# Retention transposes of keys, values and outputs gathered: one group for both heads of a pair, two PSUM tiles at a time

## The chip, the cores and the metric

The kernel runs on one core of one Trainium2 chip. The metric is the device time of one launch in microseconds (us). Three runs of the kernel before took 2369.28, 2370.20 and 2370.94 us; the median is 2370.2 us.

## The reference, cut to what matters

Two layers of a recurrent decoder run over 320 tokens at once: a prompt of 256 and 8 sequences of 8. Each layer normalises x, projects it with one wide matrix, runs three branches on the result (a diagonal state space model, a gated linear recurrence, a retention), multiplies each by its gate, projects and merges them. The change lies in the retention alone, which works in chunks of 128 tokens:

```
def step(r, inp):                       # one chunk; 8 heads of 128
    qc, kc, vc = inp
    sc = einsum('bihd,bjhd->bhij', qc, kc) * dmask
    inner = einsum('bhij,bjhe->bihe', sc, vc)
    cross = einsum('bihd,bhde->bihe', qc, r) * xi
    r_new = r * g_chunk + einsum('bjhd,bjhe->bhde', kc * zeta, vc)
    return r_new, inner + cross
# then each head's output is normalised over its 128 channels and multiplied by gn_g
y_ret = o * silu(z_ret)                 # goes into the next projection
```

The projections leave keys and values with channels on the partitions. The sums over tokens need tokens there, and so keys, values and, after the normalisation, outputs are transposed on TensorE (PE).

## The kernel before, in words

**The main stream.** All projections are one stream of matmuls, written out by `stream` (L1310). A weight chunk of 512 x 256 comes by DMA into `raw`; `prep` (L1339) splits half a chunk into a high part `whi` on ScalarE (ACT, L125) and a rest `wlo` on VectorE (DVE, L98); each 128 x 128 block is then multiplied three times (L1436 to L1438), accumulating in a PSUM tile `pt`. One half chunk is a step: 12 matmuls of 320 columns. `whi` and `wlo` have four buffers each, and `prep` is three steps ahead in the stages told of here, so the split of a step can begin only when PE has finished the step that held its buffer.

**The side work.** Everything else is written as Python generators. After each step `self.step()` lets them write their next piece into the same five in-order queues (PE, DVE, ACT, GpSimd called POOL, and SP, which issues nearly all DMAs). `yield` lets a generator rest one step and go on in the one after; `yield 0` goes on at once, unless the modelled load of DVE or ACT has run too far ahead (`BEHIND`). Which instructions stand beside which is thus fixed when the program is built.

**PSUM.** `pt` has two buffers of two banks. All side work shares four banks of [128, 512] (`ps()`, L181, pool `pside`): the tiles take the four in turn. A tile can be written only when every reader of the tile four before it is done, whichever of the two was written into the queues first.

**The retention** of a layer goes by four pairs of heads, m = 0 to 3. `ret_qk` (L884) rotates q and k: a copy with swapped halves comes back by DMA as `rsw`. `ret_heads` (L955) multiplies keys with queries into two side tiles (L973 to L977), DVE masks them into `scs` and `rsc` (L982 to L988), the keys of each head are transposed (L997) and scaled by DVE into `rkt` (L1000), the keys of the sample group likewise (`rp4`, `rkz`). `ret_v` (L910) transposes the values. Then come score times value, the normalisation, and the transposes of the outputs (`ron`, L1079), one head and then the other, with a yield between. `ret_state` (L1089) updates the states `r0` with matmuls L1112 and a DVE instruction each (L1116).

Of the kernel before, what the change touches and what calls it, by code (L numbers as in the profile page):

```python
# [15 lines left out]
OP = mybir.AluOpType  # L16
# [24 lines left out]
K_ZP, K_ZS, K_GP, K_G2, K_LO = 0, 16, 24, 48, 72  # L41
# [37 lines left out]
class Program:  # L79
# [830 lines left out]
    def ret_v(self, l, m, pt):  # L910
        nc = self.nc
        v = self.wt([128, 2, T], name="rv")
        self.mul(v, pt[:, :, :T], self.rs2())
        yield
        vd = self.vt([128, 2, 2, 64], name="rvd")
        self.copy(vd, v[:, :, None, SEQ:].to_broadcast([128, 2, 2, 64]))
        yield
        v4 = self.parts_of(v)
        yield
        vt = self.wt([128, 2, 2, 128], name="rvt")  # L920
        vs = self.vt([128, 2, 128], name="rvs")
        for n in range(2):
            p = self.ps()
            for c in range(2):
                nc.tensor.transpose(p[:, c * 128:(c + 1) * 128], v[:, n, c * 128:(c + 1) * 128], self.ident)
            nc.tensor.transpose(p[:, 256:384], vd[:, n].rearrange("p r t -> p (r t)"), self.ident)
            yield
            self.copy(vt[:, n].rearrange("p c e -> p (c e)"), p[:, :256])
            self.copy(vs[:, n], p[:, 256:384])
        p = self.rows_of(v4)  # L930
        yield
        v4 = self.wt([128, 512], F32R, name="rv4")
        self.copy(v4, p)
        self.stt(v4, v4.bitcast(F32), self.sm[:, K_LO + 1:K_LO + 2], p, OP.mult, OP.add)
        v4 = v4.rearrange("p (n c e) -> p n c e", n=2, c=2)
        self.ret['v', m] = (vt, vs, v4)
        self.flag['v', l, m] = True
# [17 lines left out]
    def ret_heads(self, l, m):  # L955
        nc, I, O, sm = self.nc, self.I, self.O, self.sm
# [8 lines left out]
        q, k = self.ret.pop(('q', m)), self.ret.pop(('k', m))  # L965
# [3 lines left out]
        k4 = self.parts_of(k)  # L969
        pp, sc = [], []  # L970
        for n in range(2):
            p = self.ps()
# [3 lines left out]
        p = pp[0][:, 384:]  # L976
# [3 lines left out]
        for n in range(2):  # L980
            r = slice(n * 64, n * 64 + 64)
# [3 lines left out]
        for n in range(2):  # L985
            t = self.vt([128, 384], name="rsc")
# [3 lines left out]
            yield 0  # L990
        kt = self.wt([128, 2, 2, 128], name="rkt")
        kz = self.wt([128, 2, 256], name="rkz")
        for n in range(2):
            h = 2 * m + n
            p = self.ps()
            for c in range(2):
                nc.tensor.transpose(p[:, c * 128:(c + 1) * 128], k[:, n, c * 128:(c + 1) * 128], self.ident)  # L997
            yield
            for c in range(2):
                self.ts(kt[:, n, c], p[:, c * 128:(c + 1) * 128],  # L1000
                        sm[:, K_ZP + 2 * h + c:K_ZP + 2 * h + c + 1], OP.mult)
        p = self.rows_of(k4)
        yield
        for n in range(2):
            h = 2 * m + n
            self.ts(kz[:, n], p[:, n * 256:n * 256 + 256], sm[:, K_ZS + h:K_ZS + h + 1], OP.mult)
        yield 0
        k4 = self.wt([128, 2, 256], F32R, name="rk4")
# [5 lines left out]
        for n in range(2):  # L1014
            r = self.rt([128, NB, 128], name="r0")
# [5 lines left out]
        vt, vs, v4 = self.ret.pop(('v', m))  # L1021
        po = []
        mv = self.pl.tile([128, 2, 3, 2], F32, name="mv", tag="mv")
        for n in range(2):
            p = self.ps()
# [28 lines left out]
        v, rs, t = (vv[:, i] for i in range(3))  # L1054
# [8 lines left out]
        on = []  # L1063
# [8 lines left out]
        while not self.flag.get(('zr', l, m)):  # L1072
            yield
        z = self.szr.pop(m)
        for n in range(2):
            h = 2 * m + n
            p = self.ps()
            for s in range(3):
                nc.tensor.transpose(p[:, s * 128:(s + 1) * 128], on[n][:, s], self.ident)  # L1079
            g = self.pcol(l, 'gn', h)  # L1080
            yield
            self.stt(z[:, n, :SEQ], p[:, :256], g, z[:, n, :SEQ], OP.mult, OP.mult)
            zs = z[:, n, SEQ:].rearrange("p (g s) -> p g s", g=4)
            self.stt(zs, p[:, 256:384].rearrange("p (g s) -> p g s", g=4)[:, :, :2 * NS], g, zs, OP.mult, OP.mult)
            yield
        yield 0
        self.y_parts(l, 1, m, z)

    def ret_state(self, l, m, kt, k4, vt, v4, r0):  # L1089
# [468 lines left out]
```

## Time and profile before

| | before |
|---|---|
| median of three runs | 2370.2 us |
| profiled execution, own time | 2368.96 us |
| its span, first to last instruction | 2367.2 us |
| PE busy | 2347.3 us, 99% |
| DVE busy | 1535.7 us, 65% |
| ACT busy | 1107.2 us, 47% |
| POOL busy | 605.7 us, 26% |

PE is busy nearly all the time, and the chain of waits that ended last runs over PE for 97% of the span. The retention stages lie at about 417 to 690 us (layer 0) and 1590 to 1870 us (layer 1). A matmul's row tells its start and a modelled length; matmuls overlap, so what one costs is the distance between starts.

### The profile page before, as it was taken

The numbers are of one execution on the slowest core, as the hardware profiler recorded it, in microseconds if no ns is written. First come the engines' busy times: TensorE is split into PE (matmuls) and PEld (weight loads), VectorE is DVE, ScalarE is ACT, GpSimd is POOL, SyncE is SP. The second block draws the span as 40 slices with busy tenths as digits, with TensorE's granted clock in tenths as the row PEclk, the third lists the DMA queues.
The fourth block names the chain that finished last, engine by engine and source line by source line (L and its number), as shares of the span: only waits on it lengthen the run. The fifth ranks groups of instructions, "written<-read, shape, count | busy, mean of one in ns | idle before, by whom it ended". The sixth has DMA issues, their size and how long they took to land.

```text
span 2367.2 us, 44419 instructions
## 1 busy us (share of the span) xinstructions
PE 2347.3 (99%) x16778; PEld 2323.5 (98%) x16778; DVE 1535.7 (65%) x2830; ACT 1107.2 (47%) x2021; POOL 605.7 (26%) x1159
## 2 busy tenths in 40 slices
PE   9999999999999999999999999999999999999997
PEld 9999999999999999999999999999999999999997
DVE  7886668676665657656557765856676656555544
ACT  6645644444443444344455564444444334444443
POOL 2020008999430000300100000699950300000011
PEclk9999999999999999999999999999999999999999
DMA  6745785455545545455646577454555554444453
GB/s 234 219 151 164 195 236 173 137 193 188 176 161 193 164 151 171 146 165 189 202 158 188 164 217 219 144 170 153 170 179 194 180 174 162 149 152 145 158 178 129
DMA packets 154311, 413.72 MB, mean 175 GB/s; under 512 B 18800, under 2 KB 60528, under 8 KB 153840
## 3 DMA queue, kind: packets, MB, share of 16 engines
q1 hardware_dynamic: 153664, 410.38, 54.6%
q8 instruction: 132, 2.16, 0.4%
q14 instruction: 83, 0.68, 0.1%
q10 hardware_dynamic: 432, 0.50, 0.1%
HBM read 373.83 MB, written 31.74 MB: 171 GB/s over the span
## 4 chain that ended last, share of the span: by engine, by line
PE 97%; DVE 2%; DMA 1%; ACT 0%; issue 0%; SPq 0%; DVEq 0%; ACTq 0%
PE pt L1436 30%; PE pt L1438 30%; PE pt L1437 30%; PE ps L679 1%; PE ps L806 1%; DVE wlo L98 1%; PE ps L582 1%; DMA raw<-w_in 0%; PE ps L1040 0%; PE ps L1112 0%; PE ps L1096 0%; PE ps L952 0%; PE ps L973 0%; PE ps L1079 0%; PE ps L671 0%
## 5 line engine op out<-in xcount | busy, mean ns | idle before, releaser
L98 DVE TENSOR_TENSOR wlo<-raw,whi 128x512 fp32r<-128x512 f32 (+1 forms) x1199 | 857.5, 725 | 746.0 <-ACT whi L125 735.7
L125 ACT ACTIVATE whi<-raw 128x512 fp32r<-128x512 f32 (+1 forms) x1199 | 744.8, 629 | 1019.2 <-PE pt L1437 847.0
L1436 PE MATMUL pt<-xh,whi 128*128 128x320 f32 x3352 | 1049.6, 313 | 1.5 <-ACT whi L125 1.0
L1437 PE MATMUL pt<-xl,whi 128*128 128x320 f32 x3352 | 1036.1, 309 | 0.8 <-DVE xl L118 0.7
L1438 PE MATMUL pt<-xh,wlo 128*128 128x320 f32 x3352 | 1036.5, 309 | 0.2 <-DVE wlo L98 0.2
L1436 PEld LDWEIGHTS pt<-xh,whi 128*128 128x128 f32 x3352 | 629.8, 188 | 7.5 <-issue 3.9
L1437 PEld LDWEIGHTS pt<-xl,whi 128*128 128x128 f32 x3352 | 630.0, 188 | 4.2 <-DVE xl L118 1.5
L1438 PEld LDWEIGHTS pt<-xh,wlo 128*128 128x128 f32 x3352 | 629.5, 188 | 0.8 <-DVE wlo L98 0.6
L1438 PE MATMUL pt<-yhl,wlo 128*128 128x320 f32 x768 | 237.4, 309 | 2.8 <-DVE wlo L98 2.8
L1436 PE MATMUL pt<-yhl,whi 128*128 128x320 f32 x768 | 238.1, 310 | 0.0
L1437 PE MATMUL pt<-yhl,whi 128*128 128x320 f32 x768 | 237.3, 309 | 0.0
L599 POOL TENSOR_TENSOR cs<-H,l2r 128x64 f32<-128x64 f32 x254 | 136.0, 535 | 239.2 <-DVE H L112 219.5
L271 POOL TENSOR_TENSOR acc<-acc,sq 128x320 f32<-128x320 f32 x28 | 25.6, 913 | 590.8 <-ACT sq L125 589.8
L1436 PE MATMUL pt<-M,whi 128*128 128x320 f32 x512 | 158.4, 309 | 0.0
L1438 PE MATMUL pt<-M,wlo 128*128 128x320 f32 x512 | 158.2, 309 | 0.0
L1437 PE MATMUL pt<-M,whi 128*128 128x320 f32 x512 | 158.2, 309 | 0.0
L1438 PEld LDWEIGHTS pt<-yhl,wlo 128*128 128x128 f32 x768 | 144.2, 188 | 3.1 <-DVE wlo L98 3.1
L1436 PEld LDWEIGHTS pt<-yhl,whi 128*128 128x128 f32 x768 | 144.2, 188 | 0.2
L1437 PEld LDWEIGHTS pt<-yhl,whi 128*128 128x128 f32 x768 | 144.2, 188 | 0.0
L600 POOL TENSOR_TENSOR cs<-H,l2i 128x64 f32<-128x64 f32 x254 | 131.8, 519 | 0.0
L601 POOL TENSOR_TENSOR cs<-cs,H 128x64 f32<-128x64 f32 x254 | 117.9, 464 | 0.0
L602 POOL TENSOR_TENSOR H<-cs,cs 128x64 f32<-128x64 f32 x254 | 107.8, 424 | 19.9
(258 smaller groups left out, 2445.5 us busy)
## 6 DMA issues: line engine op xcount, KB each, us to landing
raw<-w_in SPq DMA_DIRECT2D x447, 512.0 KB, 4.3
raw<-w_out SPq DMA_DIRECT2D x64, 512.0 KB, 4.3
raw<-wb_lru SPq DMA_DIRECT2D x32, 512.0 KB, 5.0
raw<-wb_ret SPq DMA_DIRECT2D x32, 512.0 KB, 3.7
raw<-wb_s SPq DMA_DIRECT2D x32, 512.0 KB, 3.6
r<-sret SPq DMA_DIRECT2D x16, 512.0 KB, 7.6
ret_s<-r SPq DMA_DIRECT2D x16, 512.0 KB, 3.0
raw<-w_glu SPq DMA_DIRECT2D x16, 512.0 KB, 3.5
```

The costliest lines, as they stand in the source:

```text
L98: self.nc.vector.tensor_tensor(o, a, b, op=op)
L125: self.nc.scalar.activation(o, a, f, **k)
L271: self.nc.gpsimd.tensor_tensor(self.acc, self.acc, sq, op=OP.add)
L582: self.nc.tensor.matmul(pp[g][:, a * HN:(a + 1) * HN], wst[:, a, g * 128:(g + 1) * 128], ust[:, 2 * a + g], start=True, stop=True, skip_gr ...
L599: g.tensor_tensor(t1, old, lr, op=OP.mult)
L600: g.tensor_tensor(t2, self.swap(old), li, op=OP.mult)
L601: g.tensor_tensor(t1, t1, new, op=OP.add)
L602: g.tensor_tensor(new, t1, t2, op=OP.add)
L679: nc.tensor.matmul(o[q * 32:(q + 1) * 32], w[:, c, m], H[:, q0 + m, c, col:col + HN], start=col == 1 and c == 0, stop=c == 1, tile_positio ...
L1436: nc.tensor.matmul(o, wh[:, cs], xh, start=k == 0, stop=False)
L1437: nc.tensor.matmul(o, wh[:, cs], xl, start=False, stop=False)
L1438: nc.tensor.matmul(o, wl[:, cs], xh, start=False, stop=k == nk - 1)
```

## The change

The values of both heads go into one PSUM tile and their sample rows into a second, allocated together; the keys of both heads go into one tile, and the sample keys into a second, written right behind; the outputs of both heads go into two tiles in one group. The reads stand behind one yield in place of two or three. No arithmetic changes: the same 24 transposes per pair. The copies of the values to SBUF become one of 512 and one of 256 columns, from two of 256 and two of 128.

```
         vs = self.vt([128, 2, 128], name="rvs")
-        for n in range(2):
-            p = self.ps()
-            for c in range(2):
-                nc.tensor.transpose(p[:, c * 128:(c + 1) * 128], v[:, n, c * 128:(c + 1) * 128], self.ident)
-            nc.tensor.transpose(p[:, 256:384], vd[:, n].rearrange("p r t -> p (r t)"), self.ident)
-            yield
-            self.copy(vt[:, n].rearrange("p c e -> p (c e)"), p[:, :256])
-            self.copy(vs[:, n], p[:, 256:384])
+        p, pd = self.rows_of(v), self.ps()
+        for n in range(2):
+            nc.tensor.transpose(pd[:, n * 128:(n + 1) * 128], vd[:, n].rearrange("p r t -> p (r t)"), self.ident)
+        yield
+        self.copy(vt.rearrange("p n c e -> p (n c e)"), p)
+        self.copy(vs.rearrange("p n e -> p (n e)"), pd[:, :256])
+        yield
         p = self.rows_of(v4)
...
-        for n in range(2):
-            h = 2 * m + n
-            p = self.ps()
+        pk, p = self.rows_of(k), self.rows_of(k4)
+        yield
+        for n in range(2):
             for c in range(2):
-                nc.tensor.transpose(p[:, c * 128:(c + 1) * 128], k[:, n, c * 128:(c + 1) * 128], self.ident)
-            yield
-            for c in range(2):
-                self.ts(kt[:, n, c], p[:, c * 128:(c + 1) * 128],
-                        sm[:, K_ZP + 2 * h + c:K_ZP + 2 * h + c + 1], OP.mult)
-        p = self.rows_of(k4)
-        yield
+                i = 2 * (2 * m + n) + c
+                self.ts(kt[:, n, c], pk[:, n * 256 + c * 128:n * 256 + (c + 1) * 128],
+                        sm[:, K_ZP + i:K_ZP + i + 1], OP.mult)
+            yield 0
...
-        for n in range(2):
-            h = 2 * m + n
-            p = self.ps()
+        pp = [self.ps(), self.ps()]
+        for n in range(2):
             for s in range(3):
-                nc.tensor.transpose(p[:, s * 128:(s + 1) * 128], on[n][:, s], self.ident)
-            g = self.pcol(l, 'gn', h)
-            yield
+                nc.tensor.transpose(pp[n][:, s * 128:(s + 1) * 128], on[n][:, s], self.ident)
+        yield
+        for n in range(2):
+            p, g = pp[n], self.pcol(l, 'gn', 2 * m + n)
             self.stt(z[:, n, :SEQ], p[:, :256], g, z[:, n, :SEQ], OP.mult, OP.mult)
...
-            yield
-        yield 0
+            yield 0
+        yield
         self.y_parts(l, 1, m, z)
```

**On PE, third pair (m = 2) of layer 0, before.** From the score products to the sample keys; `ps_` tiles are side tiles in the order in which they take the four banks, and the main matmuls between are left out.

```order
L973 MATMUL ps_7343<-ra_6962,ra_7141 128x256 [waits DVE_49]
L973 MATMUL ps_7346<-ra_6962,ra_7141 128x256 [waits PE_49]
...
L1112 MATMUL ps_7368<-vbd_5307,rk4_6823 128x512
...
L1112 MATMUL ps_7419<-vbd_5307,rk4_6823 128x512 [waits DVE_49,PE_49]
...
L997 MATMUL ps_7441<-ident_507,ra_7141 128x128 [waits DVE_49,PE_49]
...
L925 MATMUL ps_7462<-ident_507,rv_7318 128x128 [waits DVE_49]
...
L997 MATMUL ps_7489<-ident_507,ra_7141 128x128 [waits DVE_49]
```

The keys of the two heads (L997) stand two steps apart, each with a tile of its own, and the values (L925) between them. Tile 7441 takes the bank of 7343, and 7462 that of 7346.

**The same place after** (L951 are transposes by `rows_of`, L924 those of the sample values, L972 the score products, L1108 the state matmuls).

```order
L972 MATMUL ps_7376<-ra_6952,ra_7132 128x256
L972 MATMUL ps_7379<-ra_6952,ra_7132 128x256 [waits PE_49]
...
L1108 MATMUL ps_7383<-vbd_5307,rk4_6817 128x512 [waits PE_49]
...
L951 MATMUL ps_7432<-ident_507,ra_7132 128x128 x4
L951 MATMUL ps_7437<-ident_507,rp4_7373 128x128 [waits DVE_49,PE_49,Activation_49]
...
L1108 MATMUL ps_7443<-vbd_5307,rk4_6817 128x512 [waits DVE_49]
...
L951 MATMUL ps_7463<-ident_507,rv_7312 128x128 [waits DVE_49]
L951 MATMUL ps_7463<-ident_507,rv_7312 128x128 x3
L924 MATMUL ps_7468<-ident_507,rvd_7353 128x128 [waits DVE_49]
```

Both heads' keys, the sample keys and a state matmul now stand in one group, two steps behind the score products, and the values one step behind that. In turns of four, 7437 takes the bank of 7376, 7443 that of 7379, 7463 that of 7383, and 7468, the sample values, that of 7432, the keys.

**On DVE, the same place, before:** the masking of the scores and the first scaling of keys (`rkt`), with the splits `wlo` of the main stream between.

```order
L98 TENSOR_TENSOR rsc_7393<-ps_7343,rdm_7212 128x128
L98 TENSOR_TENSOR wlo_7397<-raw_7320,whi_7396 128x512
L98 TENSOR_TENSOR rsc_7412<-ps_7346,rdm_7212 128x256
L98 TENSOR_TENSOR rsc_7412<-ps_7346,rdm_7212 128x128
L118 SCALAR_TENSOR_TENSOR r0_6828<-r0_6828,ps_7368 128x512
L98 TENSOR_TENSOR wlo_7424<-raw_7320,whi_7423 128x512
L98 TENSOR_TENSOR wlo_7445<-raw_7370,whi_7444 128x512
L118 SCALAR_TENSOR_TENSOR r0_6828<-r0_6828,ps_7419 128x512
L98 TENSOR_TENSOR wlo_7472<-raw_7370,whi_7471 128x512
L112 TENSOR_SCALAR rkt_7439<-ps_7441,sm_508 128x128 x2
```

Two instructions read a tile of keys, four steps' splits after the scores.

**The same place after.**

```order
L98 TENSOR_TENSOR rsc_7424<-ps_7376,rdm_7200 128x256
L98 TENSOR_TENSOR rsc_7424<-ps_7376,rdm_7200 128x128
L98 TENSOR_TENSOR rsc_7427<-ps_7379,rdm_7200 128x256
L98 TENSOR_TENSOR rsc_7427<-ps_7379,rdm_7200 128x128
L118 SCALAR_TENSOR_TENSOR r0_6822<-r0_6822,ps_7383 128x512
L98 TENSOR_TENSOR wlo_7446<-raw_7355,whi_7445 128x512
L98 TENSOR_TENSOR wlo_7475<-raw_7355,whi_7474 128x512
L112 TENSOR_SCALAR rkt_7430<-ps_7432,sm_508 128x128 x4
```

The four readings of the keys' tile stand behind the splits of the two steps that follow the scores, in one run.

## Rows read from the trace of the kernel before

**Rows 1.** Page, parts 1 and 4: busy time; chain that ended last.

```profile
PE 2347.3 (99%) x16778; PEld 2323.5 (98%) x16778; DVE 1535.7 (65%) x2830; ACT 1107.2 (47%) x2021; POOL 605.7 (26%) x1159
...
PE 97%; DVE 2%; DMA 1%; ACT 0%; issue 0%; SPq 0%; DVEq 0%; ACTq 0%
```

**Rows 2.** Waits of PE, whole run: total us, times, longest.

```profile
PE pt L1438 <- DVE wlo L98: 3.0, 2, 2.8
...
PE ps L582 <- ACT H L125: 0.2, 1, 0.2
```

**Rows 3.** Timeline of PE, keys of one head: start, us, instruction.

```profile
422.10 0.31 PE L1436 MATMUL pt<-xh,whi 128*128 128x320 f32 x1
...
422.39 0.31 PE L1438 MATMUL pt<-xh,wlo 128*128 128x320 f32 x1
422.54 0.38 PE L997 MATMUL ps<-ident,ra 128*128 128x128 f32 x2
...
422.91 0.30 PE L1437 MATMUL pt<-xl,whi 128*128 128x320 f32 x1
```

**Rows 4.** Timeline of PE, a group of four transposes.

```profile
430.19 0.31 PE L1438 MATMUL pt<-xh,wlo 128*128 128x320 f32 x1
430.34 0.60 PE L952 MATMUL ps<-ident,rp 128*128 128x128 f32 x4
...
430.92 0.31 PE L1437 MATMUL pt<-xl,whi 128*128 128x320 f32 x1
```

**Rows 5.** Timelines of PE, ACT and DVE at the values, m = 2.

```profile
558.27 0.31 PE L1437 MATMUL pt<-xl,whi 128*128 128x320 f32 x1
...
558.57 0.38 PE L925 MATMUL ps<-ident,rv 128*128 128x128 f32 x2
```

**Rows 6.** The same stretch, ACT and then DVE.

```profile
558.61 0.63 ACT L125 ACTIVATE whi<-raw 128x512 fp32r<-128x512 f32 x1 [1.35 <-PE pt L1437]
...
558.28 0.68 DVE L118 SCALAR_TENSOR_TENSOR r<-r,ps 128x512 f32<-128x512 f32 x1
559.28 0.69 DVE L98 TENSOR_TENSOR wlo<-raw,whi 128x512 fp32r<-128x512 f32 x1 [0.32 <-ACT whi L125]
559.89 0.60 DVE L112 TENSOR_SCALAR rkt<-ps,sm 128x128 f32<-128x128 f32 x2
```

**Rows 7.** Lines of DVE by form: busy us, mean ns.

```profile
L112 DVE TENSOR_SCALAR rkt<-ps,sm 128x128 f32<-128x128 f32 x32 | 9.6, 341 | 0.0
```

**Rows 8.** Timeline of DVE at the scores, m = 0.

```profile
421.56 0.69 DVE L98 TENSOR_TENSOR wlo<-raw,whi 128x512 fp32r<-128x512 f32 x1 [2.57 <-ACT whi L125]
422.17 0.45 DVE L98 TENSOR_TENSOR scs<-ps,rdms 64x64 f32<-64x64 f32 x2
422.63 1.15 DVE L98 TENSOR_TENSOR rsc<-ps,rdm 128x256 f32<-128x256 f32 x4
```

**Rows 9.** Timeline of DVE at the scores, m = 1.

```profile
487.80 0.95 DVE L98 TENSOR_TENSOR yhl<-z,yhl 128x640 fp32r<-128x640 f32 x1
...
489.14 0.62 DVE L98 TENSOR_TENSOR rsc<-ps,rdm 128x256 f32<-128x256 f32 x2
```

**Rows 10.** Timeline of SP, the DMA issue behind an output transpose.

```profile
601.96 0.47 SPq L892 DMA_DIRECT2D rsw<-rraw  x1
```

**Rows 11.** Timeline of DVE behind that DMA.

```profile
606.85 0.83 DVE L98 TENSOR_TENSOR rsw<-rsw,ropr 128x640 f32<-128x640 f32 x1 [4.04 <-DMA rsw<-rraw]
607.59 0.68 DVE L118 SCALAR_TENSOR_TENSOR r<-r,ps 128x512 f32<-128x512 f32 x1
608.19 0.87 DVE L98 TENSOR_TENSOR wlo<-raw,whi 128x512 fp32r<-128x512 f32 x1
```

**Rows 12.** Timeline of PE, output transposes and the use of that split.

```profile
601.40 0.49 PE L1079 MATMUL ps<-ident,ron 128*128 128x128 f32 x3
...
609.64 0.31 PE L1438 MATMUL pt<-xh,wlo 128*128 128x320 f32 x1
```

**Rows 13.** Windows, granted clock (third column from the right) behind PE's longest wait.

```profile
953.00:960.00 7.00, 6.11 (x40) 5.84 (x41) 5.67 (x6) 2.73 (x5) 6.92 (x5) 1.00 0.25 75
```

## The prediction

> **What bounds the kernel now.** I read the page's busy times and its chain first: PE is busy for 2347.3 of 2367.2 us, and the chain runs over PE for 97% of the span [rows 1]. The other engines have room, so the time changes only if PE gets other work or has to wait. The second view is the list of PE's waits: seven rows, from 3.0 us down to 0.2 us, and none of them is for a side tile of the retention [rows 2]. So before, each retention group found its PSUM bank free when PE came to it, and there is no wait to remove. The third view is PE's timeline at the transposes, for what an interruption of the main stream costs. The last are the timelines of ACT, DVE and SP there, which tell when the readers of a bank are done, measured against the PE instruction that would want it.
>
> **The grouping itself.** Before, a pair of heads interrupts the main stream eight times: values 3, 3 and 4 transposes, keys 2, 2 and 4, outputs 3 and 3. After, four times: 6, 4, 8 and 6. No transpose is removed, so all that can be saved is a fixed cost of an interruption, 4 x 8 pairs = 32 times. Main matmuls start 0.145 us apart (422.10 to 422.39 are two of them). Two transposes stretch 422.39 to 422.91, 0.52 us, which is 0.23 more than two such distances [rows 3]; four stretch 430.19 to 430.92, 0.73 us, 0.44 more [rows 4]. The difference is 0.21 for two transposes, 0.105 each, and the fixed part 0.23 - 0.21 = 0.02 us, at the rows' own rounding. The saving is so between 0 and 32 x 0.03 = 1 us; I take 0.3. ACT and DVE do fewer and longer reads, but neither bounds.
>
> The Trainium skill speaks of this price: TensorE: Matmul & The Clock Gate, in the part on PE-mode transpose, puts one 128 x 128 transpose at about 275 ns in a kernel, most of it the latency of reading SBUF. By that each interruption would be dear and merging would pay; the spacing above shows the latency hidden behind the neighbours.
>
> **The bank of the keys.** This is the large term. Four side banks go round, and two tiles at a time go round faster. For m = 2 and 3 the order after has score products (two tiles), a state tile, keys, sample keys, a state tile, values, sample values: the eighth tile takes the fourth's bank, so the transposes of the sample values (L924) wait until DVE has read the keys' tile, with four TENSOR_SCALARs. PE reaches the values one step behind the keys, but DVE has those four two steps behind them, after a split `wlo` whose `whi` can begin only when PE has finished the step ahead of the values. All is measured in the trace at that very point. PE comes to the values at 558.57 [rows 5]. Only then does ACT get its buffer: 558.61 to 559.24; the split on DVE follows at 559.28, and the TENSOR_SCALARs behind it start at 559.89 [rows 6]. Two take 0.60 and one 0.341 us [rows 6, 7], so each further one adds 0.26, and four end at 559.89 + 0.34 + 3 x 0.26 = 561.01. A handover takes 0.03 to 0.04 us (558.58 to 558.61, 559.24 to 559.28) [rows 5, 6]; with 0.05 PE may go on at 561.06. It has meanwhile done the four transposes of the values, 0.44 us, and waits from 559.01: 2.05 us. Queued behind it on PE is the whole main stream, so all of that counts. Two pairs in two layers: 4 x 2.05 = 8.2 us. Lower bound: were the split not ahead, DVE, free at 558.96 [rows 6], would finish four at 560.08 and PE would wait 1.1 us, 4.4 in all; upper: with one 0.95 us subtract of `yhl` [rows 9] ahead, 3.0 us, 12 in all. I take the middle, which is the nearest to a row.
>
> The Trainium skill warns of such a thing: Perfetto Trace Analysis, under optimizing Scalar/DVE operations, says that where those engines are not saturated but cause bubbles elsewhere, breaking instructions up may let work complete sooner. The change does the contrary: a bank frees after four reads where it did after two. By that rule two reads instead of four would cut each such wait by 0.52 us.
>
> **The banks of the scores.** In the same pairs the sample keys take the bank of the first score tile and a state matmul that of the second, and DVE masks both in the step in which PE gets there. The row of m = 0 has this phase: the group of keys starts at 422.54 [rows 3], DVE starts masking at 422.17, has done the first tile 0.62 us [rows 9] after 422.63, at 423.25, and both at 423.78 [rows 8]. PE would have done four transposes by 422.98, wait until 423.30, do four more to 423.74 and wait to 423.83: 0.41 us, four times 1.6 us. At m = 1 the keys take the first score tile's bank themselves, but six transposes (0.65 us) stand one step earlier, in which DVE gains: 0.11 + 0.09 = 0.2, twice 0.4 us. At m = 0 no bank comes round too early. Bounds: 0 if DVE is a split earlier, 0.95 more at each of six places if a `yhl` is ahead, 7.7 us in all; since five bare splits stand ahead of the masking there, I take the 2.0.
>
> **What is moved.** The output transposes of m = 1 and 2 stand one step later (12 x 0.145 = 1.74 us). SP's DMA of `rsw` waits for the first head's transposes, since it takes their buffer: they started at 601.40 [rows 12], it issued at 601.96 [rows 10], and DVE stood 4.04 us for it, until 606.85 [rows 11]. The split behind was done at 609.06, for a matmul at 609.64 [rows 11, 12]: a margin of 0.58. After, the DMA is 1.74 later, a state update of 0.60 (607.59 to 608.19) now stands behind the split and not ahead, and PE has three more transposes (0.33) first: 0.58 - 1.74 + 0.60 + 0.33 = -0.23. I count 0.25 us once; elsewhere the margin I read is larger. Bounds 0 and 2 us. Queued behind `rsw` on SP are weight loads, which hold a lead of several steps; the loads that wait for state writes have one chunk more ahead of them than before.
>
> **The sum.** 8.2 + 1.6 + 0.4 + 0.25 - 0.3 = 10.2 us. A wait of this length costs no clock: behind PE's wait of 2.84 us the granted clock stayed 1.00, the 2.4 GHz level [rows 2, 13]. The profiled execution took 2368.96 us (its span 2367.2 and 1.8 around it), which gives 2379.1; the median of the runs lies 1.2 higher, so the forecast for it is 2380.4 us. The bounds added up give +3.4 (4.4 - 1) and +21.7 (12 + 7.7 + 2).
>
> **Rivals.** First, not slower (no change, 2370 us): the mechanism is DVE's head start. The wait decides from the point where the four TENSOR_SCALARs end before PE has done the values, that is 2.05 us earlier than read; for that ACT's `whi` would have to run without waiting for PE. Against it: the row of that `whi` names PE as what ended its idle time [rows 6]. For it: PE had no such wait before [rows 2], the ring notwithstanding. With the scores' waits gone too the time is 2370. Second, faster: an interruption costs a latency after all. The row of two transposes has 0.38 us from the first start to the last end [rows 3], so one lasts 0.38 - 0.105 = 0.275 where it takes 0.105 of the stream; if each interruption taken away saved the rest, 32 x 0.17 = 5.4 us, 2365 us, with no wait for banks. The fixed part of 0.02 [rows 3, 4] speaks against it. That figure is the one of the page on TensorE named above. Third, slower still: DVE comes to these places late, as it did at m = 1 before, where a `yhl` of 0.95 us stood just ahead of the masking [rows 9]; 0.95 at four waits for the keys and six for the scores is 9.5, 2390 us, and half of it, 2385, if the two hide each other.
>
> **How the numbers follow.** Forecast, waits of the size read: 0.78. No change: 0.09. Faster: 0.03. Slower still: 0.10. What this kernel's measurement can tell from no change is about 0.2%, 4.7 us. The forecast's own range is 2376 to 2385; with most of the slower case taken in, 2375 to 2387 leaves out less than 0.2. Slower by over 0.2% (above 2374.9) collects the forecast and the third rival: 0.87; within 0.2%: 0.09; faster by more than 0.2%: 0.04.
>
> **What would show it.** In PE's list of waits after, a side tile written by the transposes of sample values should stand with four waits of about 2 us, released by DVE's TENSOR_SCALAR of `rkt`; a row for `rows_of` released by the masking with some 0.1 to 0.4 us; and PE's busy time in the stages unchanged. The group of eight keys should take 8 x 0.105 us plus next to nothing. Wrong would be: no wait of PE for side tiles (then the first rival), or waits on `wlo` of the main stream in the retention (then what is moved costs more than I count).

## The result and the profile after

The changed kernel takes 2389.87 us (median of 6 runs, 2386.52 to 2392.03), the kernel before 2369.99 us beside it: a ratio of 1.0085, 95% interval 1.0075 to 1.0095. It is slower, by about 20 us, where 10 had been forecast; 2389.87 lies outside the range given.

The page of the profiled execution, its span and first line (before: [rows 1]):

```profile
span 2389.7 us, 44404 instructions
...
PE 2356.5 (99%) x16778; PEld 2328.7 (97%) x16778; DVE 1533.8 (64%) x2830; ACT 1106.8 (46%) x2005; POOL 600.1 (25%) x1159
```

The span grew by 22.5 us with the same 16778 matmuls; PE's busy time grew by 9.2 us only. So most of the loss is waiting, and a part is PE slower at the same work (4.2 us in the table below). PE's list of waits after (total us, times, longest; before: [rows 2]):

```profile
PE ps L924 <- DVE rkt L112: 7.6, 4, 1.9
PE ps L951 <- DVE rsc L98: 4.4, 4, 1.6
PE pt L1434 <- DVE wlo L98: 4.2, 6, 1.9
```

The first two rows are new: side tiles (`ps`) waiting for DVE to read the tile four places before. The third was 3.0 us, 2 times before: `wlo`, which should be ready for the main stream, is late at more places. How the first two come about is seen on PE at m = 2 in layer 0, and then on ACT and DVE beside it:

```profile
558.40 0.60 PE L951 MATMUL ps<-ident,ra 128*128 128x128 f32 x4
559.67 0.63 PE L951 MATMUL ps<-ident,rp 128*128 128x128 f32 x4 [0.67 <-DVE rsc L98]
560.11 0.50 PE L1108 MATMUL ps<-vbd,rk 128*128 128x512 f32 x1
...
562.20 0.60 PE L951 MATMUL ps<-ident,rv 128*128 128x128 f32 x4
564.71 0.44 PE L924 MATMUL ps<-ident,rvd 128*128 128x128 f32 x2 [1.92 <-DVE rkt L112]
564.90 0.40 PE L1432 MATMUL pt<-xh,whi 128*128 128x320 f32 x1
```

```profile
562.25 0.63 ACT L125 ACTIVATE whi<-raw 128x512 fp32r<-128x512 f32 x1 [3.16 <-PE pt L1433]
```

```profile
558.90 1.15 DVE L98 TENSOR_TENSOR rsc<-ps,rdm 128x256 f32<-128x256 f32 x4
...
562.91 0.70 DVE L98 TENSOR_TENSOR wlo<-raw,whi 128x512 fp32r<-128x512 f32 x1 [1.49 <-ACT whi L125]
563.54 1.11 DVE L112 TENSOR_SCALAR rkt<-ps,sm 128x128 f32<-128x128 f32 x4
```

This is the chain of the prediction: PE comes to the values at 562.20, ACT's `whi` starts behind it at 562.25, the split at 562.91, the four scalings at 563.54, and PE goes on with L924 at 564.71. These rows answer to [rows 5, 6]. In the same stretch DVE masks the scores (558.90) half a microsecond after PE has come to the keys (558.40), so the sample keys wait too. ACT's rows ahead of the masking, at m = 2 and at m = 3, tell what DVE was late for:

```profile
556.00 0.63 ACT L125 ACTIVATE whi<-raw 128x512 fp32r<-128x512 f32 x1 [2.75 <-DMA raw<-w_in]
...
625.76 0.63 ACT L125 ACTIVATE whi<-raw 128x512 fp32r<-128x512 f32 x1 [3.38 <-DMA raw<-w_in]
```

ACT stood for a weight load, and DVE's splits and masks come behind ACT's.

The prediction put the clock at nothing. The windows of m = 3, layer 0 (span, then busy time of PE, its weight loads, DVE, ACT and POOL; third column from the right the granted clock), ahead of a wait's end and behind it:

```profile
632.00:635.00 3.00, 1.10 (x10) 0.86 (x8) 2.32 (x6) 0.61 (x1) 0.00 (x0) 1.00 0.00 0
635.00:640.00 5.00, 5.00 (x26) 5.00 (x25) 1.43 (x2) 1.57 (x4) 0.00 (x0) 0.66 0.84 227
```

PE was busy for 1.10 of 3.00 us, and right behind it the granted clock is 0.66 on the mean of the window: full speed (2.4 GHz) for a part and the level of 1.2 GHz for the rest. In PE's timeline there the main matmuls start further apart:

```profile
636.48 0.47 PE L1432 MATMUL pt<-xh,whi 128*128 128x320 f32 x1
636.75 0.47 PE L1433 MATMUL pt<-xl,whi 128*128 128x320 f32 x1
```

That is 0.27 us instead of 0.147. Some 12 matmuls go by at this pace, 12 x 0.12 = 1.4 us, and such a stretch stands at three places in the retention: 635.5, 1748.2 and 1819.9 us.

What the same six transposes take without a wait stands in e10 below (values alone grouped), from 558.38 to 558.95:

```profile
558.38 0.60 PE L951 MATMUL ps<-ident,rv 128*128 128x128 f32 x4
558.81 0.38 PE L924 MATMUL ps<-ident,rvd 128*128 128x128 f32 x2
558.95 0.40 PE L1435 MATMUL pt<-xh,whi 128*128 128x320 f32 x1
```

Where the 22.5 us are, from the distances between matmul starts, after less before:

| where | us |
|---|---|
| values: from the first transpose to the next main matmul 2.70 us (562.20 to 564.90), where the same six take 0.57 without a wait (e10); 4 x 2.13 | +8.5 |
| keys with the tiles behind them: waits for the masked scores, 5.4 at m = 2 and 3, 0.7 at m = 1 | +6.1 |
| three stretches at the lower clock | +4.2 |
| main stream waiting for a late `wlo` (four places, 0.3 to 0.7, and 0.1 behind each) | +2.5 |
| left over: 0.3 outside the retention, the rest in small delays inside it | +1.2 |

### The profile page after: what moved, and what is told of

Read it like the earlier page. It is cut to its first block, busy times and chain, and to the rows that moved or that the text cites. A ratio compares the mean times of both kernels' runs of the same rounds, so it can differ in the third digit from the quotient of the medians.

```text
span 2389.7 us, 44404 instructions
## 1 busy us (share of the span) xinstructions
PE 2356.5 (99%) x16778; PEld 2328.7 (97%) x16778; DVE 1533.8 (64%) x2830; ACT 1106.8 (46%) x2005; POOL 600.1 (25%) x1159
## 5 line engine op out<-in xcount | busy, mean ns | idle before, releaser
L599 POOL TENSOR_TENSOR cs<-H,l2r 128x64 f32<-128x64 f32 x254 | 126.1, 496 | 239.3 <-DVE H L112 219.5
L600 POOL TENSOR_TENSOR cs<-H,l2i 128x64 f32<-128x64 f32 x254 | 126.0, 496 | 0.0
L602 POOL TENSOR_TENSOR H<-cs,cs 128x64 f32<-128x64 f32 x254 | 120.3, 474 | 19.9
```

The lines of the kernel that those rows point to most:

```text
L599: g.tensor_tensor(t1, old, lr, op=OP.mult)
L600: g.tensor_tensor(t2, self.swap(old), li, op=OP.mult)
L602: g.tensor_tensor(new, t1, t2, op=OP.add)
```

## The experiments

The first idea (A) was the prediction's: waits for banks, with late loads and the clock on top. Its rivals: each grouping has a price of its own (B), or SP's queue is what counts (C).

**e1 to e3: one of the three groups undone.** The edit is the hunk of that group in the change, taken back:

```
e1  -        p, pd = self.rows_of(v), self.ps()
    +        for n in range(2):
    +            p = self.ps()
    ...
e2  -        pk, p = self.rows_of(k), self.rows_of(k4)
    +        for n in range(2):
    ...
e3  -        pp = [self.ps(), self.ps()]
    +        for n in range(2):
    +            p = self.ps()
    ...
```

> The changed kernel with the transposes of the values back as before (per head: two of v and one of vd in one tile, a step each); keys and outputs stay grouped. Theory A (PE waits for side banks, where two tiles at a time go round the ring of four): the tile of the sample values no longer follows the keys' tile by four places in the same step, so the four waits of about 2.1 us for rkt go (8.6 us); the waits for the two masked score tiles (some 6 us) stay. If the three falls of the clock (4.2 us) need both kinds of wait close together they go too: 2377; if not: 2381. Theory B (each grouping has a price of its own, a third of the 20 us each): 2383. Theory C (what counts is that SP's queue is later, with ret_s ahead of the weight loads): no gain, 2387 or more.

> The changed kernel with the transposes of the keys back as before (per head, two transposes and a step each, then the sample keys); values and outputs stay grouped. Theory A: no tile follows the keys' tile by four places within a step (8.6 us gone); only one of the two score tiles, not both, is still wanted in the step of its masking, by the state matmul (about 1 us at four places instead of 6 in all); no falls of the clock (4.2): 2390 - 8.6 - 2 to 4 - 4.2 = 2373 to 2375. Theory B: 2383. Theory C: 2387 or more.

> The changed kernel with the transposes of the outputs back as before (a head a step); keys and values stay grouped. Theory A: in this order the masking stands two splits earlier on DVE, and the ring stands one tile otherwise, so that the sample values follow a tile of the state update and not the keys; only the second score tile can be waited for, by the sample keys: 2370 to 2374. It says then that no one grouping but their meeting makes the waits. Theory B: 2383. Theory C: the DMA of rsw is back at its old step, so the late splits (2.5 us) go, the waits for banks stay: 2387.

Measured against before: e1 2378.01 us (1.0038, 1.0025 to 1.005); e2 2378.29 us (1.0037, 1.0024 to 1.0049); e3 2371.26 us (1.0006, 0.9997 to 1.0015). So undoing one gives back 11.9, 11.6 and 18.6 us of 20: the three don't add up, against B, and SP's queue alone is not it, against C. The waits of PE in e1, then e3:

```profile
PE ps L952 <- DVE rsc L98: 4.9, 4, 2.3
PE pt L1435 <- DVE wlo L98: 4.6, 5, 2.8
```

```profile
PE pt L1434 <- DVE wlo L98: 2.8, 3, 1.9
PE ps L951 <- DVE rsc L98: 2.2, 4, 1.1
```

In e1 the row for `rkt` is gone and the others stand, and one fall of the clock, of some 1 us, is left in its retention. So the 11.9 us are roughly the 8.5 of the keys' bank and 3 of the clock, and the time lies between A's two figures. In e2 it is gone too, but the first score tile is waited for 4.0 us in all, by the state matmul; I had put 2373 to 2375, so A was right in kind and too hopeful by 3 to 5 us. e3 came inside A's range: with the outputs as before, keys and values grouped cost next to nothing.

**e5 and e9: the outputs alone, in two ways.** Both are the kernel before with the third hunk of the change alone. In e9 DVE's products with `z` stand in two steps:

```
e9       for n in range(2):
             p, g = pp[n], self.pcol(l, 'gn', 2 * m + n)
             ...
    -        yield 0
    -    yield
    +        yield
    +    yield 0
```

> The kernel before with only the output transposes grouped (six in a step, then the four products with z in one step of DVE); keys and values as before. Theory A2 (after the three undoings: the four products with z fall into the step of the add of rsw, DVE's step is then full, and the score products of the next pair start a step, 24 matmuls, later, while the keys stay where they are, so the masking is still running when PE wants the score tiles' banks): the first score tile is waited for by the state matmul, about 1 us at four places, and splits come late in the main stream at four places for 2 to 2.5 us, without any two-tile group of keys or values: 2376 to 2378. Theory D (the grouped tiles of keys and values use up the ring, whatever DVE does; the outputs alone are harmless): 2369 to 2371.

> The kernel before with only the output transposes grouped, as in e5, but DVE's products with z of the two heads in two steps. Theory A2 (e5 lost its 8.6 us because four products with z in one step push the next pair's score products a step later): the score products are back at their place, no tile is wanted in the step of its masking, no late splits: 2368 to 2371. Rival (six output transposes in a row, or two tiles taken at once, are what costs): 2376 to 2380 again.

Measured: e5 2378.09 us (1.0038, 1.0026 to 1.0051), e9 2370.79 us (1.0008, 0.9999 to 1.0017). PE runs the same grouped transposes in both; the place of two DVE instructions, and of the making of `yhl` that stands behind them, makes 7 us. DVE's timeline of e5 and of e9 at the same point:

```profile
546.32 1.25 DVE L118 SCALAR_TENSOR_TENSOR z<-ps,pv,z 128x256 f32<-128x256 f32 x4
547.49 0.95 DVE L98 TENSOR_TENSOR ra<-ra,rsw 128x640 f32<-128x640 f32 x1
```

```profile
542.80 0.66 DVE L118 SCALAR_TENSOR_TENSOR z<-ps,pv,z 128x256 f32<-128x256 f32 x2
...
544.27 0.98 DVE L98 TENSOR_TENSOR ra<-ra,rsw 128x640 f32<-128x640 f32 x1
...
546.39 0.67 DVE L118 SCALAR_TENSOR_TENSOR z<-ps,pv,z 128x256 f32<-128x256 f32 x2
```

In e5 all four products stand in the step of the add that ends the rotation of the next pair's keys and queries. Behind that add is a `yield 0`, which by the code goes on at once only if DVE's modelled load allows it: the planner has 3.0 us there in e5, above its bound of 2.4 (`BEHIND`), and 1.9 in e9. The pair's score products come 24 main matmuls later in e5 than in e9 or before, while its keys stand where they stood before (in e9 they come 12 earlier). PE's side work in e5, and then in e9:

```profile
552.58 0.59 PE L973 MATMUL ps<-ra 128*128 128x256 f32 x2
...
557.87 0.38 PE L997 MATMUL ps<-ident,ra 128*128 128x128 f32 x2
559.23 0.47 PE L1112 MATMUL ps<-vbd,rk 128*128 128x512 f32 x1 [0.99 <-DVE rsc L98]
```

```profile
548.15 0.59 PE L973 MATMUL ps<-ra 128*128 128x256 f32 x2
...
555.18 0.38 PE L997 MATMUL ps<-ident,ra 128*128 128x128 f32 x2
555.32 0.48 PE L1112 MATMUL ps<-vbd,rk 128*128 128x512 f32 x1
```

From the scores to the keys there are 7.0 us in e9 and 5.3 in e5, and only in e5 is the tile wanted here before DVE has masked it (e9's whole list has 0.2 us of that, once). In the change the same shift does a second thing: the state matmul that stood ahead of the keys (554.59, with the keys at 556.58, before) stands behind them (560.11). It takes a bank there, and so the sample values come to stand exactly four tiles behind the keys. That is why e3, with keys and values grouped, has no wait for `rkt`.

**e10 and e11: values alone, keys alone** (the first or second hunk of the change on the kernel before).

> The kernel before with only the transposes of the values grouped. Theory A2: no reader of a bank is near, so only the grouping itself is left, eight interruptions fewer: 2368.5 to 2370.5, no wait for a side tile. Rival (latency saved per interruption, 0.17 us each): 1.4 us less, 2368. Rival (two tiles at a time always cost): 2373 or more.

> The kernel before with only the transposes of the keys grouped. Theory A2: the sample keys follow the second score tile by four places in a step in which it has just been masked: waits up to about 1 us at some of four places, as in e3: 2370 to 2372. Rival (keys alone make the waits for rkt): 2378 or more.

Measured: e10 2369.93 us (1.0002, 0.9993 to 1.0011), e11 2371.17 us (1.0009, 1.0 to 1.0018). Eight interruptions fewer save nothing that can be measured. The times alone could hide a saving, since e10's profile has one new wait for a side tile (0.5 us) and a fall of the clock behind a wait of 2.80 us, shown further on, which the profile before lacks. The retention of layer 1 has neither: between the same two main matmuls there lie 279.99 us before (1590.03 to 1870.01), 280.03 in e10 (1591.08 to 1871.11) and 279.97 in e9, with four interruptions fewer in each of the two; at 0.17 us each it would be 0.7 less. The parts alone cost 8.6, 0.5 and 1.8 us; together 20.

**e6 and e7: the change with two steps for the products; e7 also with a rest ahead of the sample values.** e6 has the edit of e9 on the changed kernel; e7 adds:

```
    -        p, pd = self.rows_of(v), self.ps()
    +        p = self.rows_of(v)
    +        yield
    +        pd = self.ps()
```

> The changed kernel whole, all transposes grouped as they are, but with DVE's products with z of the two heads in two steps instead of one (the rest of a step behind each head in place of the one behind both). Theory A2: the score products start at their old place again (24 matmuls earlier), the masks are done a step before PE wants the banks, but the keys move up too, by 12 matmuls; left are a wait for the second score tile and 0.3 to 0.5 us for rkt, each at four places, and no late splits: 2371 to 2374, no fall of the clock in the retention. Theory D: the ring is as short as ever: 2385 to 2390.

> As the run before (products with z in two steps), and the sample values' transposes stand one step behind those of the values; every group of transposes of the change is kept. Theory A2: keys stand at their old place, every bank is read at least a step before PE wants it, no wait for a side tile in the retention at all: 2368 to 2371, the time before; what an interruption saves, 0.3 us, can't be seen. Rival (grouping saves something once the waits are gone, by the latency of an interruption): 2364 to 2366. Theory D: 2378 or more, since keys and sample keys still take two tiles at once.

Measured: e6 2376.32 us (1.0032, 1.002 to 1.0044), e7 2392.78 us (1.0098, 1.0084 to 1.0112). A `yield` and a `yield 0` exchanged give back 13.5 of the 20 us with every transpose still grouped, and in e6's profiled execution no fall of the clock is left in the retention. The median is some 2 us above my range. The profiled execution took 2374.27 us, at the range's edge; in it the values' groups are still 0.3 to 0.5 us too long, and the keys' groups with the state matmul take up to 1.5 us more than needed. What the median has more is not known. e7 is a miss. I had followed the ring at one pair only; at the others the rest pushes the tile towards other readers, as its waits of PE show:

```profile
PE ps L926 <- DVE rkt L112: 5.2, 4, 1.3
PE ps L953 <- DVE rsc L98: 2.4, 5, 0.8
PE ps L1110 <- DVE r L118: 2.2, 4, 0.5
```

Several kinds of tile now wait a little each, and `wlo` is late again (6.0 us in all). A rest does not cure a ring of four; it chooses who meets whom.

**e4 and e8: the state writes off SP's queue.** In the change a write `ret_s` stands on SP until 550.36 and weight loads stand behind it. The edit, in e8 with `nc.scalar`:

```
    -            nc.sync.dma_start(O['ret_s'][l, h], r0[n])
    +            nc.gpsimd.dma_start(O['ret_s'][l, h], r0[n])
```

> The changed kernel whole, but the writes of the states ret_s are issued by GpSimd instead of by SP, so that weight loads no longer stand behind them while they wait for the state update. Theory A with late loads as the reason that the scores' waits came out three times as long as forecast: ACT's splits whi no longer wait for the load of raw, DVE masks 1 to 2 us earlier; the scores' waits shrink from 6.1 to the 2.0 forecast, the late splits in the main stream from 2.5 to 0.3, and the falls of the clock go with them where the shortened waits don't suffice: 2380 to 2384; the four waits for rkt stay at 2 us. Theory A without that (DVE late for its own order of work): 2388 to 2390. Theory C (SP's queue is all): 2372.

> The changed kernel whole, the writes of ret_s issued by ACT instead of by SP (GpSimd was the wrong place: the writes stood in its chain of small operations and held that up). Theory A, with late weight loads as what makes the scores' waits 6.1 us: ACT's splits no longer wait for raw ahead of the masking, the scores' waits shrink to 2 to 3 us, late splits and falls of the clock with them; the four waits for rkt stay: 2380 to 2385. Rival (DVE late by its own order of work, or the loads are late for another reason): 2388 to 2391. Rival (ACT stands for DVE's state update at each write, 48 times): above 2392.

Measured: e4 2538.88 us (1.0715, 1.0701 to 1.073), e8 2399.56 us (1.0128, 1.0114 to 1.0142). Neither time answers, since each edit has a price of its own; the traces do. In e4 POOL itself stood for the states, and PE for the loads of the next states (`r<-sret`):

```profile
POOL ret_s L1113 <- DVE r L118: 391.3, 12, 54.5
...
PE ps L1036 <- DMA r<-sret: 149.6, 4, 87.8
```

These 149.6 us are about what e4 lost against the change (149). The four stops lie in m = 1. From 625 to 651 us PE is busy without a gap again, and then comes to the keys of m = 2; PE, then DVE:

```profile
651.48 0.60 PE L951 MATMUL ps<-ident,ra 128*128 128x128 f32 x4
652.28 0.63 PE L951 MATMUL ps<-ident,rp 128*128 128x128 f32 x4 [0.20 <-ACT whi L125]
```

```profile
651.51 1.15 DVE L98 TENSOR_TENSOR rsc<-ps,rdm 128x256 f32<-128x256 f32 x4
```

DVE masks 0.03 us behind PE's keys, in place of 0.50. At all four places the keys' groups lose 0.47 us, 1.9 in all instead of 5.4, and no wait of ACT for a weight load stands in the 8 us ahead of the masks. The four waits for `rkt` stay, 7.6 us, and late splits in the retention go from four to two. e8 has the same 0.03 us (562.91 against 562.88) and the same 1.9 us, and lost its time elsewhere. ACT, then PE at m = 2 of layer 0:

```profile
551.30 1.69 ACT L125 ACTIVATE vbd<-rv 32x256 fp32r<-32x256 f32 x4 [4.00 <-DVE r L118]
```

```profile
553.70 0.42 PE L1432 MATMUL pt<-xh,whi 128*128 128x320 f32 x1 [1.63 <-ACT whi L125]
```

ACT stood 4.00 us for a state write, and PE 1.63 for ACT, as the rival with times above 2392 had it. That alone brings PE later to the keys and would help DVE; in e4 nothing of the kind stands within 26 us ahead of these keys. So two runs with different side effects agree: the scores' waits grew from some 1.9 us to 5.4 because weight loads stood on SP behind a state write. That write issues at 549.2 to 550.4 in the change, e1, e2 and e5, which have the four products in one step, and at 545.1 to 546.3 before and in e3, e6, e9, e10 and e11.

**e12: the changed kernel once more.**

> The changed kernel once more, for its clock. If a wait of 2 us by itself brings the granted clock down, the same falls stand at the same places as in the first profile: behind the values of m = 3 in the first layer and of m = 2 and 3 in the second, and none at m = 2 of the first. If the length does not decide, the list of falls differs from one execution to the next while the waits stay the same to 0.1 us.

It took 2388.75 us. The four waits for `rkt` are the same (7.6 us, 4 times, in both profiles). The windows just behind the four, first profile and then this one:

```profile
564.90:568.30 3.40, 3.40 (x25) 3.40 (x25) 1.19 (x3) 1.39 (x3) 3.09 (x9) 1.00 0.73 206
634.60:638.00 3.40, 3.40 (x17) 3.40 (x17) 0.45 (x2) 0.75 (x2) 0.00 (x0) 0.63 0.69 196
1748.10:1751.50 3.40, 3.40 (x15) 3.40 (x15) 0.38 (x1) 0.10 (x1) 3.05 (x10) 0.51 0.73 195
1819.20:1822.60 3.40, 3.40 (x17) 3.40 (x16) 0.35 (x2) 0.70 (x2) 0.00 (x0) 0.60 0.70 200
```

```profile
565.20:568.60 3.40, 3.40 (x25) 3.40 (x25) 1.19 (x3) 1.39 (x3) 3.09 (x9) 1.00 0.75 201
633.90:637.30 3.40, 3.40 (x25) 3.40 (x25) 1.18 (x3) 1.39 (x3) 0.00 (x0) 1.00 0.71 195
1745.80:1749.20 3.40, 3.40 (x15) 3.40 (x15) 0.34 (x1) 0.18 (x1) 3.09 (x10) 0.52 0.65 193
1816.40:1819.80 3.40, 3.40 (x18) 3.40 (x17) 0.76 (x2) 1.08 (x3) 0.00 (x0) 0.67 0.67 196
```

The clock fell three times in one and twice in the other, behind waits of one length: as far as these runs show, the length of the wait does not decide whether a fall comes. Nor do the keys' waits ahead of it: these are 1.45 us at m = 3 of layer 0 in the first profile and 0.88 in this one, but in this one m = 2 has 0.95 us in both layers, with no fall in the first and a fall in the second.

## Why the prediction was half right

**The grouping itself: right.** It was put at 0 to 1 us saved; e10 has 0.5 us more, within its interval of nothing, and the distances in layer 1 leave no room for the rival by which each interruption costs 0.17 us of latency. The Trainium skill's figure of some 275 ns for a transpose (TensorE: Matmul & The Clock Gate, the part on PE-mode transpose) is not what one costs in this stream: the six of e10 take 0.57 us to the next main matmul.

**The bank of the keys: right in place and size.** 8.2 us forecast, 8.5 found: four waits for L924 released by `rkt`, each 2.1 us, through `whi`, split and scalings in the order read. e1 takes it away alone.

**The banks of the scores: mis-sized.** Place and kind were right, the size 2.0 and found 6.1. The phase was taken from m = 0, where DVE began `rsc` 0.09 us behind PE's keys [rows 3, 8]. At m = 2 it began 0.50 us behind them (558.90 against 558.40), at m = 3 1.1 us (628.63 against 627.52). With 0.03 us in e4 and e8 the four places cost 1.9 us, near the 1.6 forecast for them. So the step that failed is one that the prediction named and put at nothing: the weight loads queued on SP, which were to "hold a lead of several steps" and have only one chunk more ahead of them. At m = 2 and 3 that lead was used up; ACT stood 2.75 and 3.38 us for them. The bound of 7.7 held the size.

**What is moved: mis-sized.** The late split was found in one place and counted once, 0.25 us; it comes at four places with 0.3 to 0.7 each, 2.5 us with what follows; the prediction had named such waits as a sign that it counted too little. e5 has it with only the outputs grouped, e9 not at all. Its bound of 2 us was too low, since it was drawn for one place.

**A wait of this length costs no clock: wrong.** That was the step which failed outright, 4.2 us. It rested on one wait of 2.84 us in one execution [rows 2, 13]. The same wait stands in e10, in PE's timeline, with another window behind it:

```profile
953.83 0.63 PE L1437 MATMUL pt<-yhl,wlo 128*128 128x320 f32 x1 [2.80 <-DVE wlo L98]
```

```profile
954.50:961.00 6.50, 6.50 (x38) 6.50 (x38) 5.17 (x5) 2.91 (x5) 6.42 (x6) 0.82 0.28 86
```

Of the ten profiles in which that wait is about 3 us, seven show a fall of the clock behind it, and the kernel before happens to be one of the three that don't. The Trainium skill says of the monitor that sets the clock (TensorE: Matmul & The Clock Gate, Part 1, on the clock gate) that it runs on its own, without regard to when a kernel starts, so that counts of slow matmuls vary from run to run. The two profiles of the changed kernel agree, with three falls and two.

The sum then: 10.2 forecast, and 0.3 + 4.1 + 2.2 + 4.2 more by these steps, 21.0 of the 22.5 us; the rest is in the 0.3 us of saving that did not come and in the last row of the table. The rival "slower still" had the right time, 2390, by luck: its mechanism, a `yhl` just ahead of DVE's work at the waits, stands at none of the rows shown, and a late load was there in its place.

What the prediction did not see at all was the cause behind its own terms. It took the new order as given and priced the waits in it. That the order came from four DVE instructions in one step, and not from the groups on PE, was shown only by e9 and e6; most of the keys' and values' waits are the price of the output hunk meeting the other two. Not all: e6 still costs 6.8 us.

What stays open: what decides at which wait the clock falls, and what e6 loses beside the waits in its profile. No version tried beats the kernel before.

## What to carry to other kernels

Where PE is busy all the time and transposes stream at their spacing, grouping them saved nothing here; look instead at who reads the tile that a bank held before, at every place and not at one, since a ring of four meets other readers after each shift. A change that gathers DVE's work into one step can move the next stage's start through the planner, and that may cost more than the edit one was pricing. It can also move a write that stands ahead of loads in one queue, so read the loads' lead at the new place. And a single row at full clock behind a wait is no proof that such waits are free: count over several executions, and put 1.4 us per wait, as seen here, into the upper bound.

## What the runs showed of the hardware

- A fall of the granted clock to 1.2 GHz cost about 1.4 us of a dense stream (12 matmuls at 267 instead of 147 ns), and behind waits of the same length it came in some executions and not in others.
- State writes issued by GpSimd that had to wait for DVE made GpSimd stand for 391.3 us in all (e4), PE for 149.6 us behind them, and the kernel 149 us slower than with the writes on SP.
- ACT stood 2.75 and 3.38 us for weight loads that were queued on SP behind a state write; with the write on another queue the masks came 0.03 us behind PE's keys in place of 0.50 and 1.1 (e4, e8).
